# A layer's modulation vector: dot products on VectorE during the projections, or matmuls on TensorE during the recurrent chain

## The chip, the cores and the metric

The kernel runs on one core of a Trainium2 chip. TensorE (PE) multiplies matrices into the eight banks of PSUM, VectorE (DVE), ScalarE (ACT) and GpSimd (POOL) work element by element, and 16 DMA engines move data. Each engine takes its own instructions strictly in order and waits on semaphores. SyncE (SP), ACT and POOL issue DMAs, each from its own queue of instructions. The metric is the device time of one execution in microseconds; lower is better.

## What is computed

The reference is one step of a two-layer network on 640 tokens (128 context tokens, 512 latent tokens) of width 1024. In each layer, for both kinds of tokens with the same weights:

```
mod = silu(cvec) @ mod_w + mod_b
sh1, sc1, g1, sh2, sc2, g2 = split(mod, 6)
h = rmsnorm(x, norm1) * (1 + sc1) + sh1
x = x + g1 * token_mixing(h)
h = rmsnorm(x, norm2) * (1 + sc2) + sh2
x = x + g2 * peer(h)
```

`cvec` is one vector of 1024 for the context and one for the latent tokens, so `mod` is a product of two rows with a 1024 x 6144 matrix: 48 blocks of 128 output columns a layer. Blocks 0 to 7 are sh1, 8 to 15 sc1, 16 to 23 g1, 24 to 31 sh2, 32 to 39 sc2, 40 to 47 g2. `token_mixing` projects h to the inputs of four recurrent mixers (RWKV-7, Mamba-2 SSD, mLSTM, RG-LRU), runs each forward and backward, and multiplies the four results by `w_out`. `peer` is a product-key mixture of single-neuron experts. g1 is first needed in the output projection, sh2 and sc2 in the norm behind it.

## The kernel before

Everything is laid out with features on the 128 partitions and tokens along the free dimension. The Python code is one long program; a planner sorts its instructions for each engine. It follows the written order as a priority, moves an instruction ahead when its data and its buffer are there and the earlier ones have to wait, and judges that by its own estimate of durations. `high_priority()` gives a block a place ahead of what was written before it. A tile of a later pool can lie over the memory of an earlier, closed pool; then its first use waits until the tiles below are released.

For the first layer the work comes in these stages:

- Head (to about 50 us). `mod_head` makes sh1 by matmuls: the two modulation rows (`cct`, 128 x 8 x 2) are the stationary operand, the weights the moving one (L368). The two result rows are copied out and turned into columns of `modv` by small transposes (L374). sc1 is made by dot products.
- Projections (to about 390 us). 29 blocks of 128 columns of `w_in` go through `proj`: a 512 KB load, a split into a high and a low part (ACT and POOL), 48 matmuls into two tiles of the pool `psw` (three PSUM banks), and an eviction. Between the 4th and the 29th projection `proj` also emits 24 blocks of the modulation, 16 to 39: `mod_dot` loads 512 KB from SP's queue and DVE takes two dot products with the broadcast rows (L351).
- RWKV preparation, at high priority among the projections: `rw_prep` for both directions, `rw_inv` (62 pairs of small DVE operations a direction), `rw_merge`. Its results go to DRAM.
- The recurrent chain, also at high priority. `chain` makes four generators: context and latent tokens, forward and backward. The loop `while gens` calls each once; one round is called a tick here. A call sends one chunk of 64 tokens through (a step): small matmuls L1228 and L1231, an ACT copy L1233, L1236, two DVE operations, L1245 and L1249. The first tick only loads. Context steps, two in each direction, take PSUM from `psw`; latent steps, eight in each direction, from `ps` (three banks). 20 steps in all. Tiles come back from DRAM by SP's queue (L1195, L1197, L1202).
- RG-LRU, the tail of RWKV, mLSTM and SSD are written behind the chain and fill its gaps when they can. At that point the PSUM pools `ps`, `psw` and `pss` (3 + 3 + 2 banks) are closed and `pst`, `ps` and two `pss` (3 + 1 + 2 + 2) opened over the same eight banks. Then `out_norm`: the output projection in two halves (L1421 to L1423) and the second norm.
- `peer`, from about 720 us to 2500 us with the other blocks of the modulation as dot products in `dense`. The second layer is like the first, without a modulation of its own.

Of the kernel before, what the change touches and what calls it, by code (L numbers as in the profile page):

```python
# [9 lines left out]
F32 = mybir.dt.float32  # L10
# [18 lines left out]
P = 128  # L29
D = 1024  # L30
KC = 8
# [93 lines left out]
def prep(x):  # L125
    f = {k: np.asarray(v) for k, v in x.items()}
    o = {}
    xt = np.concatenate([f["x_prompt"][0], f["x_sample"][0]], 0).T
    o["xt"] = np.ascontiguousarray(xt.reshape(KC, P, T).transpose(1, 0, 2))
    cc = np.stack([f["c_ctx"], f["c"][0]], 1)  # L130
    o["cc"] = cc.T.reshape(1, 2 * D)
    o["cct"] = cc.reshape(KC, P, 2).transpose(1, 0, 2)
    o["modf"] = f["mod_w"][0, :, :D].reshape(KC, P, D).transpose(1, 0, 2)
    L = 2
    modw, win, wout, wq, pv = [], [], [], [], []
    rb, lruw, k12, st_rw, st_ss, st_ml = [], [], [], [], [], []
    for l in range(L):
        modw.append(f["mod_w"][l].T.reshape(48, P, D))
        w = f["w_in"][l]
        g = np.zeros((D, P), np.float32)  # L140
# [54 lines left out]
        for j, nm in enumerate(("lru_wr", "lru_wi")):  # L195
            for d in range(2):
                for h in range(4):
                    q = 64 * (h % 2)
# [57 lines left out]
class Kern:  # L256
# [66 lines left out]

    def init_cs(self, pool):
        nc = self.nc
        cc = pool.tile([P, KC, 2], F32)
        nc.scalar.dma_start(cc, self.I["cct"])
        cg = pool.tile([P, KC, 2], F32)
        nc.scalar.activation(cg, cc, AF.Sigmoid)
        nc.vector.tensor_mul(cc, cc, cg)  # L330
        self.cct = cc
        cs = self.cs_tile(pool, self.I["cc"])
        sg = pool.tile([P, 2, D], F32, name="csg")
        nc.scalar.activation(sg, cs, AF.Sigmoid)
        nc.vector.tensor_mul(cs, cs, sg)
        nc.scalar.dma_start(self.csd, cs[:1].rearrange("p s k -> p (s k)"))
# [21 lines left out]
    def mod_head(self):  # L358
        nc = self.nc
        with self.pool("modp", 6) as mp, self.pool("csr") as cp:  # L360
            cc = self.cct
            row = cp.tile([2, D], F32)
            ps = [self.psw.tile([P, 512], F32, name="mm")[:2] for g in range(2)]
            for k in range(KC):
                w = mp.tile([P, D], F32, name="modf", bufs=4)
                nc.sync.dma_start(w, self.I["modf"][:, k])
                for g in range(2):
                    nc.tensor.matmul(ps[g], cc[:, k], w[:, g * 512:(g + 1) * 512], start=k == 0, stop=k == KC - 1)  # L368
                self.mod_dot(0, 8 + k, mp, self.junk)
            for g in range(2):  # L370
                nc.scalar.copy(row[:, g * 512:(g + 1) * 512], ps[g])
            pt = self.small()[:, :2 * KC].rearrange("p (k s) -> p k s", s=2)
            for k in range(KC):
                nc.tensor.transpose(pt[:, k], row[:, k * P:(k + 1) * P], self.ident[:2, :2])  # L374
            nc.scalar.copy(self.modv[0][:, :, :8], pt.rearrange("p k s -> p s k"))
        self.mod_bias(0, 0, 16)

    def mod_scale(self, l, j):
        nc = self.nc
        if l == 0 and j:  # L380
            self.mod_bias(0, 24, 40)
        o, nm = ((8, "norm1"), (32, "norm2"))[j]
        s0, n = PV[nm]
        for s in range(2):
            nc.vector.scalar_tensor_tensor(self.a1[l][:, j, s], self.modv[l][:, s, o:o + 8], 1.0,
                                           self.pvs[l][:, s0:s0 + n], op0=ALU.add, op1=ALU.mult)
# [66 lines left out]
    def proj(self, src, hh, hl, k0=0, k1=KC):  # L453
        nc = self.nc
        n = k1 - k0
        w = self.wp.tile([P, n, P], F32, name="w")
        nc.sync.dma_start(w, src[:, k0:k1])
        wh = self.wp.tile([P, n, P], F32R, name="wh")
        wl = self.wp.tile([P, n, P], F32R, name="wl")
        self.split(wh, wl, w, self.nc.gpsimd)  # L460
        pairs = []
        for k in range(n):
            pairs += [(wh[:, k], hh[:, k0 + k]), (wh[:, k], hl[:, k0 + k]), (wl[:, k], hh[:, k0 + k])]
        r = self.mm(pairs, pool=self.psw)
        self.nproj += 1
        n_ = max(0, min(self.nproj, 29) - 3) * 24 // 26
        while self.nproj > 3 and self.nmod < n_:
            self.nmod += 1
            self.mod_dot(*self.modq.pop(0), self.wp, self.junk, self.norm_dve, bufs=1)
        return r  # L470

    def proj2(self, l, c0, out, func=AF.Copy, scale=1.0):
# [798 lines left out]
    def mixing(self, l, es):  # L1271
        nc = self.nc
        with ExitStack() as e1:
# [5 lines left out]
            with ExitStack() as e2, ExitStack() as er:  # L1279
# [11 lines left out]
                with ExitStack() as ep:  # L1291
# [4 lines left out]
                    def chain(psc, nm):  # L1296
                        cp = ech.enter_context(self.pool("cp"))
                        cx = ech.enter_context(self.pool("cx", 3))
                        stt = cx.tile([P, 2, 2, 64], F32, name="stt", bufs=1)
                        nc.sync.dma_start(stt, self.I["st_rw"][l])  # L1300
                        Y = cp.tile([P, 2, T], F32, name="Y")
                        gens = []
                        for part in range(2):
                            for d in range(2):
                                bufs = []
                                for z in range(2):
                                    t = cp.tile([P, 2, 2, 64], F32, name=f"S{part}{d}{z}")
                                    nc.gpsimd.memset(t, 0.0)
                                    bufs.append(t)
                                gens.append(self.rw_chain(l, d, part, stt, PC, bufs, Y, cx, psc if part else self.psw, nm))  # L1310
                        self.done = set()
                        while gens:
                            gens = [g for g in gens if next(g, None)]
                        return Y, cx

                    with self.pool("nt", 2) as np_, self.pool("csp") as cp:
# [12 lines left out]
                    with ExitStack() as e3:  # L1329
                        en3 = e3.enter_context  # L1330
                        ra = en3(self.pool("rwa"))
                        r, k, kk, th, la, rb, omk = self.rwkv_front(l, ra)
                        evp = enr(self.pool("evp", 2, "right"))
                        rv = en3(self.pool("rwv"))
                        for w in STAGES[l]:
# [8 lines left out]
                            else:  # L1344
                                n, c, kw = {"k": ("k", W_MLK, dict(scale=0.125)), "q": ("q", W_MLQ, {}), "v": ("v", W_MLV, {}),
                                            "o": ("o", W_MLO, dict(func=AF.Sigmoid)), "g": ("lg", W_LRG, dict(func=AF.Gelu))}[w]
# [17 lines left out]
                        with self.tc.high_priority():  # L1364
                            Y, cx = chain(self.ps, "mm")
# [470 lines left out]
    def run(self):  # L1836
        with ExitStack() as es:
            start(self, es)
            self.xstack = ExitStack()
            self.nproj = self.nmod = 0  # L1840
            self.alt = []
            self.modq = [(0, q) for q in range(16, 48)] + [(1, q) for q in range(48)]
            for l in range(2):
                self.pv = self.pvs[l]
                with ExitStack() as ps:
                    self.mixing(l, ps)
                    self.peer(l)
            self.final()
            self.xstack.close()
# [72 lines left out]
```

## Time and profile before

| | |
|---|---|
| Runs | 4816.89, 4827.43, 4833.49 us, median 4827.43 |
| The profiled execution's own time | 4815.13 us |
| Its span | 4813.4 us |
| Busy share of the span: PE, DVE, POOL, ACT | 92%, 73%, 50%, 38% |
| Mean granted clock of TensorE | 0.944 |
| Moved by DMA | 1025.95 MB, mean 213 GB/s |

A line of a profile gives the engine, the operation, output and inputs by tile name, the shape, how often, busy time and mean duration, and then how long the engine stood idle just before these instructions and what released it. PE's f32 matmul of the program is two instructions in the trace. PEld is the load of the stationary operand, which overlaps PE. The granted clock is a share of full speed: 1.00 is 2.4 GHz, 0.50 is 1.2 GHz; a value between them in a stretch is a mixture of the two.

### The profile page before, as it was taken

Reading aid. Unit: us, or ns where it says so; the run is one execution under the profiler, and the core shown is the slowest. Engines: PE = TensorE matmul, PEld = TensorE weight load, DVE = VectorE, ACT = ScalarE, POOL = GpSimd, SP = SyncE. Lnnn points to the kernel's source line nnn. Section 1 sums busy time; section 2 is a strip of 40 time slices with the busy share of each in tenths; the row PEclk is TensorE's granted clock in tenths of the full one; section 3 lists DMA queues with packets and bytes.
Section 4 is the critical chain, followed back from the end, with each engine's and each line's share of the span. In section 5 each row is a group of like instructions: output and inputs, shape, how many; then the busy total and the mean of one; then the engine's idle time right before and its main releaser. Section 6 shows DMA issues by size and latency. Waiting matters only on the chain. (4 is left out here: it accounts for less than half of the span.)

```text
span 4813.4 us, 64776 instructions
## 1 busy us (share of the span) xinstructions
PE 4434.1 (92%) x23050; PEld 3667.5 (76%) x23050; DVE 3512.6 (73%) x6243; ACT 1816.1 (38%) x3359; POOL 2390.1 (50%) x1295
## 2 busy tenths in 40 slices
PE   7998879999999999899989899799999999999997
PEld 5786668788888877677767877687878888877675
DVE  7784569978765699986777757699786665445676
ACT  3432423345555522222233233334545553222222
POOL 2220233465665566676642213324755665665564
PEclk8996689999999999999999996899999999999999
DMA  5576332358788788888843664323788886777785
GB/s 194 181 192 183 99 128 65 123 193 272 253 277 279 250 278 295 296 284 260 292 145 117 188 197 128 116 76 122 254 255 267 263 280 228 244 257 258 256 298 182
DMA packets 504277, 1025.95 MB, mean 213 GB/s; under 512 B 80017, under 2 KB 247185, under 8 KB 502801
## 3 DMA queue, kind: packets, MB, share of 16 engines
q1 hardware_dynamic: 280112, 592.70, 38.5%
q0 software_dynamic: 75328, 275.02, 17.3%
q10 hardware_dynamic: 148514, 154.10, 9.5%
q8 instruction: 181, 2.97, 0.3%
q14 instruction: 142, 1.16, 0.1%
HBM read 841.41 MB, written 180.24 MB: 212 GB/s over the span
## 5 line engine op out<-in xcount | busy, mean ns | idle before, releaser
L1620 POOL TENSOR_TENSOR ul<-u,uh 128x1024 fp32r<-128x1024 f32 x256 | 661.6, 2586 | 663.9 <-ACT uh L1619 563.6
L1745 PE MATMUL O<-q,vh 128*128 128x512 f32 x2048 | 817.7, 400 | 105.1 <-DVE q L1767 104.4
L1626 PE MATMUL S<-hh,ul 128*128 128x512 f32 x2048 | 813.8, 397 | 14.7 <-POOL ul L1620 14.7
L1746 PE MATMUL O<-qh,vl 128*128 128x512 f32 x2048 | 807.4, 395 | 19.1 <-POOL vl L1754 18.8
L1754 POOL TENSOR_TENSOR vl<-v,vh 128x1024 fp32r<-128x1024 f32 x256 | 675.1, 2638 | 300.6 <-ACT vh L1753 291.6
L1624 PE MATMUL S<-hh,uh 128*128 128x512 f32 x2048 | 813.5, 397 | 9.7 <-ACT ring L1628 9.7
L1744 PE MATMUL O<-qh,vh 128*128 128x512 f32 x2048 | 803.1, 394 | 9.4 <-ACT qh L1766 6.9
L1625 PE MATMUL S<-hl,uh 128*128 128x512 f32 x2048 | 804.1, 393 | 0.0
L1745 PEld LDWEIGHTS O<-q,vh 128*128 128x128 f32 x2048 | 389.1, 190 | 231.5 <-DVE q L1767 151.9
L1764 DVE TENSOR_TENSOR h<-h,gt 128x384 f32<-128x384 f32 x250 | 267.8, 1072 | 398.3 <-issue 288.5
L310 POOL TENSOR_TENSOR wl<-w,wh 128x1024 fp32r<-128x1024 f32 (+1 forms) x106 | 240.3, 2270 | 585.3 <-ACT wh L309 512.1
L1619 ACT CAST uh<-u 128x1024 fp32r<-128x1024 f32 x256 | 268.0, 1047 | 648.2 <-PE S L1625 327.0
L1662 DVE SCALAR_TENSOR_TENSOR junk<-row,hpr 128x1024 bf16<-128x1024 f32 x256 | 368.7, 1440 | 194.4 <-DMA row<-in_u_dram,ix 192.3
L1766 ACT CAST qh<-h 128x512 fp32r<-128x512 f32 x250 | 154.7, 619 | 850.9 <-DVE h L1765 626.1
L1746 PEld LDWEIGHTS O<-qh,vl 128*128 128x128 f32 x2048 | 389.9, 190 | 102.9 <-POOL vl L1754 25.2
L1744 PEld LDWEIGHTS O<-qh,vh 128*128 128x128 f32 x2048 | 390.2, 191 | 93.7 <-ACT qh L1766 8.1
L1626 PEld LDWEIGHTS S<-hh,ul 128*128 128x128 f32 x2048 | 387.6, 189 | 95.9 <-POOL ul L1620 16.9
L1624 PEld LDWEIGHTS S<-hh,uh 128*128 128x128 f32 x2048 | 388.3, 190 | 86.1 <-ACT ring L1628 11.9
L1625 PEld LDWEIGHTS S<-hl,uh 128*128 128x128 f32 x2048 | 387.7, 189 | 77.5
L1654 POOL DMA_INDIRECT row<-in_v_dram,ix x256 | 314.9, 1230 | 265.2 <-DVE hpr L1670 224.7
L296 PE MATMUL mm<-hh,wh 128*128 128x320 f32 x1184 | 382.9, 325 | 13.1 <-ACT hh L443 10.1
L296 PE MATMUL mm<-hl,wh 128*128 128x320 f32 x1184 | 384.4, 325 | 6.6 <-POOL hl L450 2.0
(449 smaller groups left out, 8430.1 us busy)
## 6 DMA issues: line engine op xcount, KB each, us to landing
u<-in_ub_dram SPq DMA_DIRECT2D x256, 512.0 KB, 4.0
v<-in_v_dram SPq DMA_DIRECT2D x256, 512.0 KB, 5.5
sd<-ring ACTq DMA_DIRECT2D x250, 256.0 KB, 3.5
h<-sd SPq DMA_DIRECT2D x250, 256.0 KB, 4.0
gd<-stg ACTq DMA_DIRECT2D x96, 512.0 KB, 6.6
gt<-gd SPq DMA_DIRECT2D x256, 192.0 KB, 3.8
modw<-in_modw_dram SPq DMA_DIRECT2D x88, 512.0 KB, 4.6
w<-in_win_dram SPq DMA_DIRECT2D x58, 512.0 KB, 4.7
```

The lines of the kernel that those rows point to most:

```text
L296: nc.tensor.matmul(t[:m, :HT], a, b[:, sl], start=k == 0, stop=k == n - 1)
L1619: pa = nc.scalar.copy(uh, u)
L1620: pp = nc.gpsimd.tensor_sub(ul, u, uh.bitcast(F32))
L1624: nc.tensor.matmul(ps, uh[:, k], xh, start=k == 0, stop=False)
L1625: nc.tensor.matmul(ps, uh[:, k], xl, start=False, stop=False)
L1626: nc.tensor.matmul(ps, ul[:, k], xh, start=False, stop=k == KC - 1)
L1654: nc.gpsimd.indirect_dma_start(out=r, out_offset=None, in_=self.I[tab], in_offset=bass.IndirectOffsetOnAxis(ap=ix[:, s:s + 1], axis=0))
L1662: nc.vector.scalar_tensor_tensor(junk, r, 1.0, hp, op0=ALU.mult, op1=ALU.mult, accum_out=act[:, s:s + 1])
L1744: nc.tensor.matmul(acc[c], vh[:, sl], qh, start=z == 0, stop=False)
L1745: nc.tensor.matmul(acc[c], vh[:, sl], q, start=False, stop=False)
L1746: return nc.tensor.matmul(acc[c], vl[:, sl], qh, start=False, stop=z == NB - 1)
L1754: pace = nc.gpsimd.tensor_sub(vl, v, vh.bitcast(F32))
```

## The change

The 24 blocks (g1, sh2, sc2 of the first layer) are no longer made by `mod_dot` in `proj`. A new generator `mod_rows` makes them like the head makes sh1: for each of the three groups it holds two PSUM tiles from `psw`, loads eight tiles of 512 KB by POOL's queue (three buffers in the chain's pool `cx`), multiplies each by two matmuls, and after the eighth copies the two rows, transposes them and writes eight columns of `modv`. Each `yield` is a step: 24 in all. The chain's loop takes three steps behind every tick, and the rest after the last one. The host lays the same weights out a second time as `modg`; `cct` moves to a pool that lives through the whole kernel. The list of blocks for `dense` is as long as it was at that point before.

```diff
+    o["modg"] = f["mod_w"][0, :, 2 * D:5 * D].reshape(KC, P, 3, D).transpose(2, 0, 1, 3)
...
-        cc = pool.tile([P, KC, 2], F32)
+        cc = self.res.tile([P, KC, 2], F32, name="cct")
...
+    def mod_rows(self, pool):
+        nc = self.nc
+        for g in range(3):
+            ps = [self.psw.tile([P, 512], F32, name="mm")[:2] for c in range(2)]
+            for k in range(KC):
+                w = pool.tile([P, D], F32, name="modg", bufs=3)
+                nc.gpsimd.dma_start(w, self.I["modg"][g, k])
+                for c in range(2):
+                    nc.tensor.matmul(ps[c], self.cct[:, k], w[:, c * 512:(c + 1) * 512], start=k == 0, stop=k == KC - 1)
+                if k < KC - 1:
+                    yield True
+            row = pool.tile([2, D], F32, name="modr", bufs=1)
+            for c in range(2):
+                nc.scalar.copy(row[:, c * 512:(c + 1) * 512], ps[c])
+            pt = self.small()[:, :2 * KC].rearrange("p (k s) -> p k s", s=2)
+            for k in range(KC):
+                nc.tensor.transpose(pt[:, k], row[:, k * P:(k + 1) * P], self.ident[:2, :2])
+            nc.scalar.copy(self.modv[0][:, :, 16 + 8 * g:24 + 8 * g], pt.rearrange("p k s -> p s k"))
+            yield True
...
-        self.nproj += 1
-        n_ = max(0, min(self.nproj, 29) - 3) * 24 // 26
-        while self.nproj > 3 and self.nmod < n_:
-            self.nmod += 1
-            self.mod_dot(*self.modq.pop(0), self.wp, self.junk, self.norm_dve, bufs=1)
         return r
...
+                        extra = self.mod_rows(cx) if l == 0 else iter(())
                         while gens:
                             gens = [g for g in gens if next(g, None)]
+                            for _ in range(3):
+                                next(extra, None)
+                        for _ in extra:
+                            pass
                         return Y, cx
...
-            self.nproj = self.nmod = 0
             self.alt = []
-            self.modq = [(0, q) for q in range(16, 48)] + [(1, q) for q in range(48)]
+            self.modq = [(0, q) for q in range(40, 48)] + [(1, q) for q in range(48)]
```

## Rows read from the trace of the kernel before

**Rows 1.** The page: busy time of each engine, and clock in 40 slices.
```profile
PE 4434.1 (92%) x23050; PEld 3667.5 (76%) x23050; DVE 3512.6 (73%) x6243; ACT 1816.1 (38%) x3359; POOL 2390.1 (50%) x1295
...
PEclk8996689999999999999999996899999999999999
```

**Rows 2.** Stretches: length, busy PE PEld DVE ACT POOL, clock, DMA share, GB/s.
```profile
60.00:392.00 332.00, 302.78 (x2153) 272.95 (x2152) 265.42 (x442) 116.61 (x204) 92.11 (x51) 0.92 0.58 169
392.00:411.50 19.50, 0.41 (x5) 0.19 (x3) 12.64 (x20) 3.51 (x6) 3.02 (x3) 0.55 0.86 234
411.50:462.00 50.50, 49.38 (x305) 36.15 (x306) 17.49 (x40) 9.32 (x20) 0.54 (x1) 0.50 0.75 235
462.00:496.00 34.00, 33.01 (x362) 24.87 (x360) 21.16 (x53) 13.47 (x27) 5.84 (x4) 0.99 0.22 69
496.00:523.00 27.00, 26.93 (x139) 20.60 (x138) 12.47 (x26) 6.67 (x13) 8.77 (x8) 0.51 0.21 69
523.00:690.00 167.00, 132.48 (x601) 102.86 (x601) 103.91 (x204) 55.59 (x89) 46.54 (x35) 0.70 0.40 123
```

**Rows 3.** PE's waits, 60 to 392 us, on DVE: total us, times, longest.
```profile
PE sm L1097 <- DVE ar L1081: 4.4, 2, 2.4
...
PE mm L296 <- DVE hl L447: 0.5, 1, 0.5
```

**Rows 4.** Groups of DVE instructions, 60 to 392 us: the dot products.
```profile
L351 DVE SCALAR_TENSOR_TENSOR junk<-modw,cs 128x1024 bf16<-128x1024 f32 x48 | 65.3, 1360 | 27.4 <-DMA modw<-in_modw_dram 27.1
```

**Rows 5.** Timeline of PEld in the head: start, length, instruction, idle before.
```profile
38.56 0.09 PEld L368 LDWEIGHTS mm<-modf,cc 128*2 128x2 f32 x2 [3.79 <-DMA modf<-in_modf_dram]
...
41.40 0.13 PEld L368 LDWEIGHTS mm<-modf,cc 128*2 128x2 f32 x1 [0.72 <-issue]
42.26 0.13 PEld L368 LDWEIGHTS mm<-modf,cc 128*2 128x2 f32 x1 [0.72 <-issue]
...
43.26 0.09 PEld L368 LDWEIGHTS mm<-modf,cc 128*2 128x2 f32 x1 [0.34 <-issue]
43.69 0.09 PEld L368 LDWEIGHTS mm<-modf,cc 128*2 128x2 f32 x1 [0.34 <-issue]
```

**Rows 6.** Groups of PE instructions, 40 to 50 us: the head's transposes.
```profile
L374 PE MATMUL sm<-cstA,row 2*128 2x2 f32 x8 | 0.8, 202 | 0.3 <-ACT row L371 0.3
```

**Rows 7.** Timeline of PE, a chain step in the first cold stretch.
```profile
436.73 0.64 PE L1228 MATMUL mm<-S,ar 128*64 128x128 f32 x2
...
441.69 0.64 PE L1228 MATMUL mm<-S,ar 128*64 128x128 f32 x2
```

**Rows 8.** Timeline of PE, a chain step in the warm stretch.
```profile
480.81 0.38 PE L1228 MATMUL mm<-S,ar 128*64 128x128 f32 x2
...
482.23 0.81 PE L296 MATMUL mm<-lx,llw 128*128 128x320 f32 x2
...
483.58 0.43 PE L1245 MATMUL mm<-ar,S 128*128 128x64 f32 x2
...
484.97 0.38 PE L1228 MATMUL mm<-S,ar 128*64 128x128 f32 x2
```

**Rows 9.** Stretches, line L1228 alone: length, PE, PEld, clock, DMA share, GB/s.
```profile
411.50:462.00 50.50, 13.20 (x40) 6.11 (x40) 0.50 0.75 235
...
496.00:523.00 27.00, 2.64 (x8) 1.24 (x8) 0.51 0.21 69
```

**Rows 10.** DMA, 395 to 445 us in 40 slices: busy tenths, GB/s.
```profile
DMA  9755848999999999999999999999799970000110
GB/s 218 182 102 168 241 145 170 129 276 404 371 304 346 320 364 406 322 290 323 316 285 315 314 300 306 320 278 279 221 279 382 320 257 22 0 0 0 26 26 0
```

**Rows 11.** Groups, 400 to 525 us: DMA issues on POOL.
```profile
L664 POOL DMA_DIRECT2D pj<-rv x2 | 1.1, 548 | 22.2 <-DVE rv L663 22.2
```

**Rows 12.** Tile lx, 380 to 480 us: min/median/max ns, first and last start.
```profile
L296 PEld LDWEIGHTS mm<-lx,llw x14: 186/189/333, 446.8 to 478.2; 128*128 128x128 f32 x14
```

**Rows 13.** Groups of PE, 411.5 to 523 us: other work inside the chain.
```profile
L296 PE MATMUL mm<-lx,llw 128*128 128x320 f32 x18 | 9.7, 631 | 0.0
...
L531 PE MATMUL sm<-cstA,k 128*128 128x128 f32 x10 | 1.7, 309 | 0.0
```

## The prediction

> **What bounds the kernel now.** First the page: TensorE is busy 92% of the span, VectorE 73% [rows 1]. That is a mean over stages, so next the table of stretches, cut at the places where the change works [rows 2]. The first layer's projections (60 to 392 us) keep PE busy 302.8 of 332 us at a clock of 0.92, DVE 265.4. The recurrent chain runs from 411.5 to about 523. PE's row is full there too, but at a granted clock of 0.50, 0.99 and 0.51: a full row at 1.2 GHz, which is not PE at its peak. Between them, from 392 to 411.5, PE does 0.41 us of work. After the chain the mLSTM, SSD and output projection run to 690 with 34.5 us of PE idle; the 4123 us behind it hold nothing that the change touches except a shift of their start.
>
> Then what PE waited for in the projections: nine of the rows name DVE, together 18.1 us, the first 4.4 and the last 0.5 [rows 3]. So PE binds this stage, and DVE is the second: 48 dot-product instructions take 65.3 us, and DVE stood idle another 27.4 us in front of them, nearly all for the weights' DMA, with the recurrence's preparation queued behind [rows 4]. DVE's queue is thus held (265.4 + 27.4) / 332 = 88% of the stretch.
>
> **The change, part by part.** (a) *Dots leave the projections.* 92.7 us of DVE queue go, and 24 loads of 512 KB with their issues leave SP's queue. PE covers most of it: what can come back is its wait for DVE, 18.1 us, or at most all of its idle time, 332 - 302.8 = 29 us. The lower end is nothing, if the next projection's weight split or eviction is late in place of DVE. I take 16: nearer to 18.1, since the dots stood in the same queue as the named releasers, but some of those waits are DVE's own work.
>
> (b) *Matmuls.* 24 steps of two f32 matmuls, each of which the trace shows as two instructions, so 96 with a 2-column stationary and 512 moving columns. The kernel has the same form in its head: they start 0.43 us apart at the upper clock (43.26 to 43.69) and 0.86 at the lower (41.40 to 42.26) [rows 5]. That is 96 x 0.43 = 41.3 us or 96 x 0.86 = 82.6. Three groups of eight small transposes add 3 x 0.8 = 2.4 [rows 6]. I take the upper clock: 43.7. Six row copies and three column copies fall to ACT, which is busy 29.5 of the chain's 111.5 us [rows 2]: nothing, as long as none stands just ahead of a chain copy.
>
> (c) *The clock of the chain.* One chunk step takes 4.96 us of PE at the lower clock (436.73 to 441.69) [rows 7]. At the upper clock the same step takes 4.16 with 1.35 of other work inside it (482.23 to 483.58), so 2.81 [rows 8]. L1228 has four instructions in a step: 40 in the first cold stretch and 8 in the last [rows 9], so 12 of the 20 steps run cold, and warming them is worth up to 12 x 2.15 = 25.8 us; the lower end is zero. In the trace the chain's steps ran at 0.99 from 462 to 496, with matmuls of the RG-LRU and mLSTM between them, and at half that before and after [rows 2, 8]; the new form itself held the upper pitch in the head [rows 5]. Three steps a tick put 5.2 us of it between every two chain ticks. I take 11 steps, -24, since the last tick has no matmuls of it left.
>
> (d) *The hole before the chain.* The generator's first steps come ahead of the chain's first matmul in the written order and need no chain data. The hole of 19.1 us [rows 2] is there to take them: none if the loads are late, eleven steps of 1.72 us if they keep coming. With three buffers and DMA engines that are nearly full I take six steps, -10.
>
> (e) *Loads.* 24 x 512 KB = 12.6 MB move from SP's queue in the projections to POOL's in the chain. The engines ran full there from about 405 to 436 at some 316 GB/s with the chain's own tiles [rows 10], so 12.6 MB are worth 40 us of them; behind 437 they have room. An issue of this kind costs POOL 0.55 us, and the one in the trace had waited 22.2 us for a conv result [rows 11]: what stands behind such a wait on POOL is late with it. I cost this at nothing in the sum, because three buffers and the idle engines behind 437 cover it; without the cover it is the slower rival below.
>
> The Trainium skill has a rule against (e): SBUF — State Buffer, "SBUF: two separate sides", says that a DMA issued from GpSimd waits for its descriptors while VectorE runs an operation that takes both of their shared ports. The page's own example stretches one DMA by about 2.5 us; as an estimate 24 of these would be 60 us of waiting spread over three buffers, which would turn the sum from faster to slower if it were all exposed. No row of before shows such a load waiting in that way; what it would do here is the late-weights rival, priced there from rows.
>
> The sum: -16 + 43.7 - 24 - 10 = -6.3 us. The profiled execution is 4815.1 us (span 4813.4, 1.7 around it), 12.3 below the median of the runs; I put the change on the median: 4827.4 - 6.3 = 4821.
>
> **Rivals.** *Faster: PE's slack is real everywhere.* DVE's relief gives all 29 us, the hole takes ten steps (-17), all 12 cold steps warm (-25.8): -29 + 43.7 - 17 - 25.8 = -28, so 4799. For it: DVE held at 88%, a clock of 0.92 in the projections [rows 2]. Against it: PE waited for DVE only 18.1 us, and the split and PE's own order remain.
>
> *Slower: the weights come late, and PE waits in order.* If the matmul at the head of PE's queue finds its weights still in flight, the chain's steps behind it wait as well, and the clock stays down. In the head of the kernel just this is seen: PE's weight load waited 3.8 us for the DMA at 38.56, and the pitch was 0.86 from 39.70 to 42.26 before it came back to 0.43 [rows 5]. By half of that (half of the matmuls at the lower clock, 62 + 2.4, half of the clock's return, -12, the same relief of -16, a hole of -10): +26, so 4853; by all of it 82.6 + 2.4 - 16 - 10 = +59, so 4886. It decides from about one step in four waiting. For it: engines already full at 405 to 436 [rows 10], and a POOL queue with long waits [rows 11]. The Trainium skill speaks for this one: TensorE: Matmul & The Clock Gate, "Loop structure matters more than you think", calls a DMA wait ahead of each matmul the case in which PE goes cold, and the rows at 38.56 agree.
>
> *Slower: PSUM banks.* The row sums hold two of the three banks of the projections' pool through the chain. The later pools lie over these banks: the RG-LRU's first matmul came at 446.8 [rows 12], 35 us into the chain, whose first ticks hold the four context steps that use the same pool. Its work and the mLSTM's inside the chain, seven groups from 9.7 to 1.7 us, together 32.7 [rows 13], would slide behind the last row sum. About half would find PE idle later (34.5 us in 523 to 690): +16, in all -6.3 + 16 = +10, so 4837; with ScalarE and VectorE links behind it up to +25.
>
> *It does not run in the chain.* The code raises the priority of the whole chain, so the planner may set the matmuls among the last projections as soon as a buffer is free. Then (d) and (c) are gone and 43.7 - 16 = +28 remain, so 4855.
>
> **How the numbers follow.** The forecast's case gets 0.41 (own range 4806 to 4838), the faster rival 0.27, late weights 0.18, banks 0.09, early placement 0.05. A measurement of this kernel can tell a change from none at about 0.3%, 14.5 us. The forecast's case gives 0.10 faster, 0.27 same and 0.04 slower; the banks give 0.04 same and 0.05 slower; late weights and early placement are slower, 0.23, and the faster rival faster, 0.27. Together faster 0.37, same 0.31, slower 0.32. The range goes from 15 us below the faster rival to between the two prices of late weights: 4784 to 4872.
>
> **What would show it.** Right for (a): no idle DVE time before dots and PE busier from 60 to 392. For (b): 96 instructions at 0.43 us; at 0.86 the clock term failed. For (c): a granted clock above 0.9 through the chain, steps near 2.8. For (d): matmuls on the new tile before the first L1228. For (e): no long PE wait for the new weights. The bank rival shows in the RG-LRU's first matmul standing behind the last row sum; early placement in new matmuls long before 390. The prediction is wrong if the output projection's first matmul is over 25 us earlier or 35 us later than now, or if the time moves behind 690.

## The result, and the profile after

The changed kernel takes 4865.3 us (median of 10 runs, 4856.2 to 4888.0); beside it the kernel before takes 4830.5 (10 runs, 4816.7 to 4848.7). The ratio is 1.0085, 95% interval 1.0062 to 1.0109: by it about 41 us slower (the two medians lie 35 apart), where 6 us faster was forecast. The profiled execution has a span of 4859.9 us, 46.5 longer than the one before.

First the page of the changed kernel: busy time, and the clock in 40 slices. Against [rows 1] DVE loses 46 us and PE gains 42.

```profile
PE 4476.4 (92%) x23170; PEld 3668.7 (75%) x23170; DVE 3466.6 (71%) x6146; ACT 1805.6 (37%) x3361; POOL 2404.7 (49%) x1319
...
PEclk9999589999999999999999896799999999999999
```

The stretches of the first layer, with the columns of [rows 2]. The chain now runs from 360.3 to 451 us and no stretch up to there is below 0.96 in clock. The hole ahead of the chain is gone, filled by projections (159 PE instructions from 337 to 360.3). The new cost is the stretch 451 to 487: the chain is over, and PE has 78 instructions, 52 of them row sums.

```profile
60.00:337.00 277.00, 260.19 (x1943) 231.91 (x1942) 184.00 (x310) 100.03 (x182) 77.68 (x46) 0.96 0.51 149
337.00:360.30 23.30, 23.30 (x159) 23.02 (x157) 12.27 (x17) 5.73 (x10) 7.05 (x6) 1.00 0.96 321
360.30:400.00 39.70, 39.34 (x331) 26.54 (x331) 21.86 (x46) 5.18 (x13) 4.56 (x5) 1.00 0.56 194
400.00:451.00 51.00, 50.39 (x412) 29.16 (x410) 27.40 (x60) 9.56 (x19) 8.14 (x12) 0.99 0.69 213
451.00:487.00 36.00, 30.86 (x78) 6.88 (x79) 10.31 (x20) 7.40 (x13) 5.40 (x10) 0.91 0.64 210
487.00:523.00 36.00, 19.36 (x120) 13.62 (x118) 22.09 (x42) 21.30 (x36) 15.50 (x11) 0.66 0.43 125
523.00:690.00 167.00, 131.83 (x624) 104.03 (x625) 94.45 (x191) 43.52 (x78) 44.37 (x35) 0.70 0.35 111
```

The tile `modg`: its matmuls and loads (minimum, median and maximum ns, first and last start), then for how long its instructions waited and who waited for them (us in total, times). The loads stand 72.5 us behind the matmuls that free their buffers; the matmuls and weight loads wait 17.4 us for the data, in 18 pieces.

```profile
L387 PE MATMUL mm<-modg,cct x96: 591/592/1057, 377.2 to 485.0; 128*2 128x512 f32 x96
L385 POOL DMA_DIRECT2D modg<-in_modg_dram x24: 540/540/722, 337.9 to 479.3; - x24
...
  PE mm L387: 72.5, 18
...
  PEld mm L387: 12.5, 10
  PE mm L387: 4.9, 8
```

PE's timeline at the end of the row sums. The RG-LRU's first matmul, at 446.8 us before [rows 12], stands directly behind the last transposes of the rows.

```profile
483.71 1.88 PE L387 MATMUL mm<-modg,cct 128*2 128x512 f32 x4 [0.53 <-DMA modg<-in_modg_dram]
485.52 0.41 PE L395 MATMUL sm<-cstA,modr 2*128 2x2 f32 x4
486.25 0.40 PE L395 MATMUL sm<-cstA,modr 2*128 2x2 f32 x4 [0.33 <-ACT modr L392]
486.59 0.81 PE L297 MATMUL mm<-lx,llw 128*128 128x320 f32 x2
```

In these two profiles all of this nearly cancels: the first score matmul of the first layer comes at 743.2 us before and 745.1 after. The second layer begins at 2473.4 and 2481.2. Of the 46.5 us between the spans the other 39 arise in the second layer, whose code the change does not touch.

### The profile page after: what moved, and what is told of

The parts are those of the page before. It is cut to its first block, busy times and chain, and to the rows that moved or that the text cites. A ratio compares the mean times of both kernels' runs of the same rounds, so it can differ in the third digit from the quotient of the medians.

```text
span 4859.9 us, 64979 instructions
## 1 busy us (share of the span) xinstructions
PE 4476.4 (92%) x23170; PEld 3668.7 (75%) x23170; DVE 3466.6 (71%) x6146; ACT 1805.6 (37%) x3361; POOL 2404.7 (49%) x1319
## 5 line engine op out<-in xcount | busy, mean ns | idle before, releaser
L1683 DVE SCALAR_TENSOR_TENSOR junk<-row,hpr 128x1024 bf16<-128x1024 f32 x256 | 357.6, 1397 | 186.0 <-DMA row<-in_u_dram,ix 180.6
```

The costliest lines, as they stand in the source:

```text
L1683: nc.vector.scalar_tensor_tensor(junk, r, 1.0, hp, op0=ALU.mult, op1=ALU.mult, accum_out=act[:, s:s + 1])
```

## The experiments

The planner sorts both layers in one pass, so the first thing compared was the order of each engine's instructions in the compiled programs. In the second layer the kernel before and the changed kernel hold the same instructions, but 963 of TensorE's 9962 places and 942 of VectorE's 2456 hold another one. In the traces the orders part behind the chain: at 2911 us TensorE has an RG-LRU matmul in the kernel before, and an mLSTM one in its place in the changed kernel. Call before's order O1 and after's O2; two more turned up, O3 and O4. Small edits in the first layer push the planner from one to the other, and so do a few memsets at the layers' border. That gives a handle: first layer and second layer's order can be set apart.

The table holds all twelve profiles, in us, by starts of instructions: the first layer's chain, its last new matmul (a transpose of the rows), its first score matmul (S1); then of the second layer the chain's length, the time from its end to the first score matmul ("tail"), and from there to the first output matmul of the dense part ("score"). The last column is the ratio to before, with its interval, from all runs; the other columns are one execution each.

| kernel | order | chain 1 | last new | S1 | chain 2 | tail 2 | score 2 | ratio |
|---|---|---|---|---|---|---|---|---|
| before | O1 | 411.5-522.0 | | 743.2 | 82.9 | 219.5 | 908.9 | 1 |
| changed | O2 | 360.3-450.6 | 486.5 | 745.1 | 85.1 | 240.8 | 918.4 | 1.0085 (1.0062-1.0109) |
| changed again (e6) | O2 | 360.0-466.3 | 503.7 | 763.6 | 85.8 | 236.4 | 920.4 | 1.0082 (1.0051-1.0113) |
| order of before (e5) | O1 | 361.9-453.8 | 489.7 | 747.3 | 82.7 | 220.2 | 906.0 | 1.0014 (0.9987-1.0040) |
| two buffers (e1) | O1 | 366.0-467.5 | 508.1 | 768.4 | 102.6 | 223.0 | 905.8 | 1.0036 (1.0011-1.0062) |
| added only (e2) | O2 | 411.2-531.0 | 528.7 | 804.3 | 102.5 | 237.0 | 920.0 | 1.0211 (1.0179-1.0243) |
| no dots (e3) | O1 | 356.7-441.9 | | 691.1 | 82.0 | 216.5 | 903.9 | 0.9924 (0.9900-0.9948) |
| third order (e4) | O3 | 402.1-499.4 | | 729.6 | 102.9 | 215.3 | 910.8 | 1.0046 (1.0018-1.0074) |
| six buffers (e7) | O4 | 362.0-483.6 | 483.9 | 771.8 | 95.6 | 233.4 | 920.0 | 1.0101 (1.0056-1.0145) |
| fourth order (e8) | O4 | 410.9-516.1 | | 738.6 | 85.4 | 231.2 | 912.3 | 1.0060 (1.0028-1.0092) |
| 16 blocks (e9) | O1 | 385.2-477.9 | 486.7 | 749.4 | 83.0 | 217.6 | 906.2 | 1.0010 (0.9986-1.0034) |
| 8 blocks (e10) | O1 | 385.7-492.0 | 455.6 | 747.0 | 82.6 | 216.2 | 909.8 | 0.9989 (0.9971-1.0006) |

### Is it the edit or the second layer's order?

**Two buffers (e1)**, which happens to give O1.

```diff
-                w = pool.tile([P, D], F32, name="modg", bufs=3)
+                w = pool.tile([P, D], F32, name="modg", bufs=2)
```

> The changed kernel with two buffers in place of three for the rows of the modulation weights. In the first layer it does the same work as the changed kernel; in the second layer each of the five engines' streams of instructions is, one by one, that of the kernel before (in the changed kernel 963 of 9962 places on TensorE and 942 of 2456 on VectorE hold another instruction). Theory A (the second layer's order of instructions costs the 46 us): first layer up to its first out-projection of the second half +0 to +8 us against before, second layer as before, sum 4830 to 4845, so +0 to +15 us. Theory B (the loss comes with the edit itself: the addresses that move with it, or the end of the first layer carried on): as the changed kernel, +30 to +45 us.

Measured: 4835.7 us, ratio 1.0036, +17 us, 2 above theory A's range and far from B's 30 to 45. Its first layer is longer than I expected of it (S1 at 768.4: with two buffers the rows end at 508.1), and it is still well under the changed kernel. The profiled execution was the longest of its runs (4867.0 against a median of 4835.7), with a cold chain in the second layer; its tail and score still fall with O1.

**Added only (e2).** The changed kernel with the five lines of before put back into `proj` (ahead of the projection's matmuls, where before has them behind) and the rows copied to a scratch tile:

```diff
...
+        while self.nproj > 3 and self.nmod < n_:
+            self.nmod += 1
+            self.mod_dot(*self.modq.pop(0), self.wp, self.junk, self.norm_dve, bufs=1)
...
-            nc.scalar.copy(self.modv[0][:, :, 16 + 8 * g:24 + 8 * g], ...)
+            nc.scalar.copy(pool.tile([P, 2, KC], F32, name="mods", bufs=1), ...)
...
```

> The kernel before with the matmuls, loads and row copies of the change added and its dot products kept (the rows go to a scratch tile, so all 24 blocks are computed twice). In the second layer its streams of instructions are those of the changed kernel. Theory A: the second layer's mixing is 25 to 35 us longer than before as in the changed kernel, and in the first layer the added TensorE work costs 10 to 45 us with no relief of VectorE; +45 to +80 us in all. Theory B (the loss sits with the removal of the dot products and what it shifts): second layer as before, +10 to +45 us.

Measured: 4923.3 us, +102 by the ratio, above the range of either theory. The tail and score of the second layer are those of O2 (theory A), but the first layer was dearer than I allowed: S1 is 61 us later than before.

**No dots (e3).**

```diff
-            self.mod_dot(*self.modq.pop(0), self.wp, self.junk, self.norm_dve, bufs=1)
+            self.modq.pop(0)
...
```

> The kernel before without the 24 blocks (neither loaded nor computed; their columns stay zero, one memset at the start). In the second layer its streams are those of the kernel before. By the prediction's terms: 16 us from VectorE in the projections, and the chain starts as early as in the changed kernel, 40 to 50 us before; the hole ahead of the chain closes. Theory A: second layer as before, sum -15 to -40 us. Theory B in the form that the removal moves addresses or times in the second layer: +0 to +30 us in spite of the relief.

Measured: 4785.4 us, ratio 0.9924, -37 us; theory A, and the second layer's tail and score are before's. The profiled execution, 4755.7 us, was the shortest of its runs; in it the first layer gains 52 us to S1. Its stretches, columns as above, hold a surprise: with no row matmul in the kernel the chain still runs at a clock of 1.00 and 0.96.

```profile
338.00:356.70 18.70, 18.70 (x128) 18.36 (x126) 10.99 (x15) 4.66 (x8) 4.82 (x2) 1.00 0.84 256
356.70:400.00 43.30, 43.30 (x406) 34.04 (x405) 21.03 (x51) 8.31 (x18) 3.55 (x3) 1.00 0.54 183
400.00:442.00 42.00, 40.06 (x385) 28.69 (x386) 27.23 (x61) 18.12 (x34) 4.18 (x3) 0.96 0.65 195
442.00:690.00 248.00, 190.66 (x968) 154.28 (x967) 162.35 (x322) 87.95 (x164) 82.74 (x67) 0.75 0.37 113
```

What is different there is that the chain starts 55 us earlier, while projections are still to be done; that this keeps the clock up was not shown (e6, below, starts its chain in the same way). Of the projections' matmuls 80 run after its first one, up to 396.5 us, and the RG-LRU's follow from 410.7; in the kernel before it is none, since the last of them starts at 380.2 and the chain at 411.5.

**Third order (e4)**: before with a steeper ramp of the dots.

```diff
-        n_ = max(0, min(self.nproj, 29) - 3) * 24 // 26
+        n_ = max(0, min(self.nproj, 29) - 3) * 24 // 24
```

> The kernel before with the 24 dot products let in a little faster, two more of them with the projections (26 in place of 24). Nothing of the change is in it. In the second layer its streams are a third order: 865 of 9962 places on TensorE and 910 of 2456 on VectorE hold another instruction than in the kernel before. Theory A: the first layer within 8 us of before, the second layer's mixing longer or shorter by 10 to 40 us between its 2700 us and its last out-projection. Theory B: within 10 us of before everywhere.

Measured: 4842.3 us, ratio 1.0046. The first layer ended 14 us earlier in the profile, more than the 8 that I expected of it; the second layer's mixing took 660.7 us in place of 644.1, but all of that stands in its chain (102.9 against 82.9), at a clock of 0.71 in place of 0.93; the last section comes back to it. Outside the chain O3 shows no price in this profile, so it speaks for neither theory. The time leaves room for one: by the ratio the run is 22 us above before in spite of the shorter first layer.

**Order of before (e5)**: the changed kernel, and at the second layer's start

```diff
                 nc.vector.memset(PC, 0.0)
+                for _ in range(6 * l):
+                    nc.vector.memset(PC, 0.0)
```

> The changed kernel, and at the start of the second layer six more memsets of PC, a small tile that is zeroed there anyway (well under 1 us in all). In the first layer it is the changed kernel instruction by instruction. They move the planner: in the second layer the streams of TensorE and ScalarE are again those of the kernel before, and VectorE's but for the memsets. Theory A (the second layer's order costs most of the loss): first layer as in the changed kernel, 743 to 750 us to the first score matmul; second layer's mixing 20 us shorter than in the changed kernel; time 0 to +15 us against before. Theory B (the loss comes with the edit, whatever the order): +30 to +45 us as the changed kernel.

**Changed again (e6)**: the changed kernel, no edit.

> The changed kernel once more, beside the others on one chip. Both theories: +30 to +50 us against before. Its second profile shows how far one stretch moves between executions of the same program: the first layer to the first score matmul within 15 us of 745, the recurrent chain of the second layer either near 85 or near 103 us (both occur among the six profiles so far), the rest of the second layer's mixing and its dense part within 5 us of the first profile.

Measured on one chip: e5 4832.7 us, ratio 1.0014 with no difference from before in its interval; e6 4871.1 us, 1.0082. Six memsets take 0.0068 of 4824.6 us, 33 us, off the changed kernel, and leave its first layer as it is. The intervals of the two ratios do not overlap, and together they leave some 20 us either way on the 33. That is theory A, and theory B has fallen. By the table the difference of O2 (three profiles) from O1 (six) is 238.1 - 218.8 = 19 us of tail and 919.6 - 906.8 = 13 us of score, 32 in all. e6's first layer ended 18.6 us from 745 where I had allowed 15. Its chain took 106.3 us where the same program had taken 90.3, and the clock of its stretches, columns as above, was lower:

```profile
360.00:386.00 26.00, 24.94 (x173) 17.62 (x173) 6.75 (x18) 2.63 (x7) 2.35 (x1) 0.60 0.70 217
386.00:426.00 40.00, 40.00 (x275) 23.55 (x273) 19.40 (x41) 4.82 (x11) 4.36 (x8) 0.96 0.60 207
426.00:466.30 40.30, 39.79 (x297) 23.07 (x296) 22.73 (x46) 7.28 (x14) 5.95 (x8) 0.83 0.42 122
```

So one profile's S1 can lie some 18 us from another's of the same program.

Where the tail loses it shows in stretches of 40 us from the chain's end on, columns as above. First e5 (O1), then the changed kernel (O2), four each. The second stretch is the difference: at 0.59 PE does 144 instructions where at 0.76 it does 191. The other profiles agree: from 40 to 80 us behind the chain's end O1's six have 191 to 207 instructions at 0.76 to 0.80, O2's three 144 to 154 at 0.59 to 0.62.

```profile
2898.70:2938.70 40.00, 34.40 (x120) 22.87 (x118) 29.12 (x54) 23.71 (x35) 14.03 (x12) 0.59 0.51 163
2938.70:2978.70 40.00, 37.73 (x191) 31.63 (x190) 27.36 (x58) 11.57 (x25) 15.91 (x13) 0.76 0.61 174
2978.70:3018.70 40.00, 40.00 (x228) 33.35 (x228) 24.73 (x69) 8.35 (x14) 12.32 (x11) 0.79 0.20 51
3018.70:3058.70 40.00, 18.89 (x115) 12.70 (x113) 22.74 (x44) 9.32 (x14) 7.22 (x4) 0.81 0.48 153
```

```profile
2908.70:2948.70 40.00, 36.00 (x112) 23.51 (x110) 26.88 (x48) 21.84 (x32) 9.54 (x7) 0.50 0.34 98
2948.70:2988.70 40.00, 34.74 (x144) 30.22 (x144) 21.52 (x49) 9.46 (x22) 13.96 (x12) 0.59 0.69 213
2988.70:3028.70 40.00, 38.31 (x206) 33.63 (x205) 30.13 (x65) 12.67 (x22) 18.25 (x15) 0.77 0.23 70
3028.70:3068.70 40.00, 27.64 (x165) 19.70 (x164) 22.09 (x48) 4.73 (x7) 7.23 (x4) 0.74 0.36 119
```

In that stretch O2 holds mLSTM matmuls where O1 already has the output projection's: the first eviction of the output projection comes 59.9 us after the chain's end in e5 and 78.5 in the changed kernel (first and last start, first e5, then the changed kernel):

```profile
L1480 DVE SCALAR_TENSOR_TENSOR x<-mm,modv,x x24: 337/408/552, 2958.5 to 3025.0; 128x128 f32<-128x128 f32 x8, 128x192 f32<-128x192 f32 x8, 128x320 f32<-128x320 f32 x8
```

```profile
L1478 DVE SCALAR_TENSOR_TENSOR x<-mm,modv,x x24: 335/404/551, 2987.2 to 3033.7; 128x128 f32<-128x128 f32 x8, 128x192 f32<-128x192 f32 x8, 128x320 f32<-128x320 f32 x8
```

In the score part, PE's waits (total us, times, longest) from the gates' scatter on, again e5 (3239 to 3419 us) and then the changed kernel (3270 to 3450), grow from 5.6 to 16.6 us (e5's lines have numbers higher by two):

```profile
PE S L1647 <- ACT ring L1651: 4.7, 2, 3.6
PE G L1628 <- DVE A L1620: 0.5, 1, 0.5
PE sm L1740 <- DVE oh L1736: 0.4, 1, 0.4
```

```profile
PE S L1647 <- POOL ul L1641: 4.6, 4, 1.8
PE G L1626 <- DVE A L1618: 4.3, 2, 4.0
PE S L1645 <- ACT ring L1649: 3.9, 1, 3.9
PE sm L1738 <- DVE oh L1734: 2.0, 1, 2.0
PE sm L1607 <- DVE e L1545: 1.8, 1, 1.8
```

In the same stretch the six profiles of O1 have 5.6 to 8.8 us of such waits and the three of O2 16.1 to 16.6.

**Fourth order (e8)** crosses over: the first layer of before, another order behind it. The edit is e5's with `8 * l`, made to the kernel before.

> The kernel before, and at the start of the second layer eight more memsets of PC (about 1 us). In the first layer it is the kernel before instruction by instruction; in the second its TensorE stream is the fourth order, that of the kernel with six buffers. Theory A: first layer as before, the second layer's mixing 10 to 30 us longer or shorter, the time with it. Theory B (orders are worth nothing): within 5 us of before.

Measured: 4847.1 us, ratio 1.0060. The first layer is before's (738.6 against 743.2). The mixing of the second took 17.4 us longer (661.5 against 644.1), 11.7 of it in the tail, and the score 3.4. Nothing but some 1 us of memsets and their effect on the order is different, so an order alone costs about 29 us by the ratio. Theory A. An order does not fix the score part to the last microsecond, though: e7, also O4, took 920.0 us there, with 16.5 us of the waits above, and e8 912.3, with 10.7. That O2 behind the first layer of before would cost its 32 us was not tried by itself.

### What do the new matmuls cost, and why?

**Six buffers (e7).** `bufs=6` in the line that e1 edits.

> The changed kernel with six buffers for the rows of the modulation weights in place of three. Theory L (the new matmuls end 36 us behind the chain because each load waits for a buffer, 72.5 us of waits of the loads on the matmuls): the last of them 20 to 30 us earlier than 485 us, the first score matmul 15 to 30 us earlier than 745. Rival (the loads are bound by what the DMA moves beside them, or the matmuls by their own 96 x 0.59 us): the last of them within 8 us of 485 us. In the second layer it has a fourth order (763 places of TensorE differ from before, 634 from the changed kernel), whose price is not known: -10 to +30 us by theory A, nothing by theory B.

Measured: 4878.0 us, ratio 1.0101. Theory L fell: the loads' wait halves, the wait for data is gone, and the last new matmul still starts at 480 us; S1 comes at 771.8, 27 us later than in the changed kernel, where 15 to 30 earlier was expected. The tile again:

```profile
L387 PE MATMUL mm<-modg,cct x96: 591/592/1034, 383.3 to 480.1; 128*2 128x512 f32 x96
L385 POOL DMA_DIRECT2D modg<-in_modg_dram x24: 537/538/572, 338.0 to 465.5; - x24
...
  PE mm L387: 35.0, 15
```

Now they stand inside the chain, which ends at 483.6 in place of 450.6 (its first 38 us have a clock of 0.73, so not all of that is theirs). So the rows of about 100 us either follow the chain or lengthen it. O4 adds its price on top.

**16 blocks (e9)**: groups 1 and 2 as rows, the first 8 blocks as dots, with e5's memsets.

```diff
-        for g in range(3):
+        for g in (1, 2):
...
-        n_ = max(0, min(self.nproj, 29) - 3) * 24 // 26
+        n_ = max(0, min(self.nproj, 29) - 3) * 8 // 26
```

> Only 16 of the 24 blocks on TensorE (the two later groups), the first 8 stay dot products on VectorE beside the projections; six more memsets of PC at the start of the second layer, so that its TensorE and ScalarE streams are those of the kernel before. In the changed kernel the new matmuls outlast the chain by 36 us (450.6 to 486.5 us) and the first matmul of the linear recurrence follows right behind the last of them. Theory T (that tail is what the 24 blocks cost too much): with a third fewer the tail goes, the last new matmul lies within 10 us of the chain's end, the chain still starts 20 to 40 us before that of the kernel before, and the first score matmul comes 10 to 30 us before 743 us; -5 to -30 us in all. Rival (the 8 dot products left cost their share of the 50 us that the kernel without any of the 24 gained, and the matmuls their share): between the kernel before and the changed kernel with the order of before, -5 to +10 us.

**8 blocks (e10)**: `(2,)` and `* 16 // 26`.

> As the kernel with 16 blocks on TensorE, with only 8 there (the last group) and 16 dot products left; the second layer's TensorE and ScalarE streams again those of the kernel before. Theory T: the new matmuls end inside the chain, no tail; the chain starts 10 to 25 us earlier than before, the first score matmul 5 to 20 us; -5 to -20 us in all. Rival: shares alike, within 6 us of before.

Measured: 4831.9 us, 1.0010, and 4819.0 us, 0.9989; neither differs from before. With a third fewer rows the last one still starts at the same time (486.7), and the chain starts 25 us later than in the changed kernel; the rows then outlast it by 9 us only, and S1 is at 749.4, no earlier than before. With a third of the rows they do end inside the chain, and S1 is at 747.0 all the same. Theory T fell, the shares hold. No division of the blocks between the engines that was tried beats the kernel before, and with before's order and three buffers none measurably loses either.

## Why the prediction was wrong, step by step

**The step that failed** is in the first part: that the 4123 us behind 690 "hold nothing that the change touches except a shift of their start". They hold some 33 of the 41 us by e5 and e6, 32 by the stretches of the table: the order in which the planner sets the second layer's instructions changed with the edit, and it alone costs that. The prediction put this at nothing, because no code there is touched. The front says that a planner sorts one long program; I took its judgement into account around the chain (the rival of early placement) and not beyond it. The condition "if the time moves behind 690" named this case without giving it a price or a chance; the other condition was not met, the output projection's first matmul coming at 579.1 us in place of 569.8.

The time of 4865 lies inside the range of 4784 to 4872 all the same. That is luck: the range reached so far for late weights, which are not what happened. With before's order the same edit measures 1.0014 (e5): +7 us, interval -6 to +19, where -6.3 was forecast. The terms behind that sum came near in size, the largest not for the reason given.

**(a) and (c), relief and clock.** Together I had -16 - 24, with the hole -50; e3, with no rows at all, measures -37 by the ratio and -52 to S1 in its profile. The size came near, the mechanism was another. VectorE's dots did not mainly hold up PE: they held up the chain's preparation. With them gone, the merges end at 337 us in place of 392 (their matmuls before, then in the changed kernel, with first and last start):

```profile
L1187 PE MATMUL mm<-Am,X x104: 269/269/472, 330.9 to 392.1; 64*64 64x128 f32 x104
```

```profile
L1203 PE MATMUL mm<-Am,X x104: 269/269/320, 279.8 to 336.9; 64*64 64x128 f32 x104
```

The chain then runs beside the last projections, in this profile at a full clock, in e6 at 0.60, 0.96 and 0.83. In e2, which keeps the dots and adds the rows, it starts at 411.2 as before. Whether VectorE's queue or the dots' loads in SP's queue held the preparation up was not separated, since e3 takes out both. I had read the 88% of VectorE's queue as cover for PE's waits [rows 3, 4], when the releaser to ask for was that of the chain's first step. Before, L1228 stood idle for a load that SP issues behind the merges' last stores:

```profile
L1228 PE MATMUL mm<-S,ar 128*64 128x128 f32 x80 | 22.4, 375 | 20.8 <-DMA ar<-sR 19.8 <-PE mm L1249 1.0
```

PE's own waits on DVE in 60 to 360 us after the change are 3.9, 1.9, 0.8 and 0.3 us, 6.9 in place of 18.1. That is 11 of the 16 us that (a) was to bring.

**(c) as written**, row matmuls that warm the chain, shows in the one profile of e2. There the chain starts as late as before, and its clock is 0.79, 0.90 and 1.00 where it was 0.50, 0.99 and 0.51 [rows 2]:

```profile
411.20:462.00 50.80, 47.59 (x312) 25.49 (x312) 17.81 (x40) 6.66 (x14) 4.79 (x9) 0.79 0.85 280
462.00:496.00 34.00, 33.88 (x235) 18.26 (x234) 6.73 (x18) 2.74 (x8) 2.69 (x5) 0.90 0.52 162
496.00:529.00 33.00, 33.00 (x202) 14.24 (x202) 5.49 (x15) 3.98 (x10) 4.30 (x8) 1.00 0.49 150
```

It buys nothing: the chain takes 119.8 us in place of 110.5, since the rows' own time stands in it.

**(b) matmuls.** 96 instructions as counted, mostly at the upper pitch of [rows 5]: four of them start and end within 1.88 us in the timeline above. In the time their price cannot be told from the 43.7 us: between e3 and e5 lie 1.0014 - 0.9924 = 0.0090, 43 us, with some 17 either way. What they hold up is more than their own durations, though. In the profiles S1 moves from 691.1 without them to 745.1, 747.3 and 763.6 with them, 54 to 72 us (in e6 with the low clock in it), and in e2 by 61. Loads and sums stretch over 109 us, outlast the chain by 36, and the RG-LRU follows behind the last. That is what the bank rival foresaw: in the seven profiles with 16 or 24 blocks of rows the first RG-LRU matmul comes 0.1 to 0.2 us behind the rows' last instruction (from 483.9 and 484.1 in e7 to 528.7 and 528.8 in e2). I had given it 0.09. It was not the data that held it in the changed kernel: the load of its input `lx` was issued at 445.9 us, and the last signal that the matmul waits for came at 450.0, 36 us ahead of it.

```profile
L704 SPq DMA_DIRECT2D lx<-pj x1: 563/563/563, 445.9 to 445.9; - x1
```

Whether the banks or the order that the planner gave PE holds it was not separated.

**(d) the hole** closed, by projections and not by rows: the first new matmul comes at 377.2, behind the chain's first.

**(e) loads.** Behind [rows 10, 11] I looked for a collision. The wait for data is 17.4 us, and in this profile the clock fell to 0.91 only in the last stretch. Late weights as I had priced them, with the clock down at half, did not happen. The Trainium skill, SBUF — State Buffer, "SBUF: two separate sides", would have POOL's loads held back during some of VectorE's operations; the runs do not show it. In e1, whose trace has the landings, the 24 loads land 3.9 us after their issue in the median, and SP's loads of the same size before took 4.6. In the changed kernel the last load was issued at 479.30 and its matmuls run from 483.71 on, 4.4 us later. The Trainium skill's TensorE: Matmul & The Clock Gate, "Loop structure matters more than you think", is borne out in direction alone: in 451 to 487, where PE waits eight times for the new weights, the clock is 0.91, and before it 0.99.

## What to carry to other kernels

Where one planner orders a whole program, compare the order of the instructions in the parts that an edit does not touch before explaining a difference, and measure the edit under the old order too; here a few memsets at a border were enough to bring that order back. To price work taken off an engine, ask what the next serial stage's first instruction waited for, not only what the busiest engine waited for. Matmuls put into another stage's gaps can occupy the program for as long as their loads and their buffers last: here 109 us, where their durations were put at 44.

## What the runs showed of the hardware

The second layer's chain has much the same instructions in all twelve profiles and takes 82.0 to 85.8 us in eight, 95.6 in one and 102.5 to 102.9 in three, whatever the order. Its row before and in e1, columns as above, shows the clock as the difference:

```profile
2815.00:2898.00 83.00, 77.29 (x754) 57.65 (x753) 48.20 (x94) 28.70 (x57) 11.52 (x7) 0.93 0.62 185
```

```profile
2842.00:2945.00 103.00, 97.13 (x757) 72.12 (x758) 47.24 (x94) 28.80 (x57) 10.27 (x7) 0.71 0.50 149
```

So 20 us go with the clock granted in one such stretch, and not with the order. Whole executions of one kernel spread as well: before went from 4800 to 4855 us over 27 runs on one chip, and of e8's twelve one with a mean clock of 0.941 took 4840 us, one at 0.929 took 4896. A single profile against a single profile could not have told 33 us from chance; stretches that agree over three and six profiles, and five rounds of times, could.
